# A two-layer trunk on one core: the first product of each MLP computed transposed, with the weights as stationary operand

## The chip, the core and the metric

The kernel is one launch on one core of a Trainium2 chip. It is written in Bass with the Tile framework: the program allocates tiles from pools, and a scheduler orders the instructions of each engine and places the waits between them. The engines that do the work are TensorE (PE in the profile; PEld are its weight loads), VectorE (DVE), ScalarE (ACT) and SyncE (SP), which issues the loads of the weights.

The metric is device time in microseconds (us) of the core. Before the change it is 2300.85 us, the median of three executions (2300.76 to 2300.91).

## The reference, cut to what matters

A sequence of 256 rows of 2048 numbers goes through two layers. Each layer adds the result of a mixer (attention of one kind or another) and then the result of an MLP. All is float32. The part that the change touches is the MLP with the norm ahead of it:

```python
def rms_norm(x, g):
    y = x * lax.rsqrt(jnp.mean(x * x, axis=-1, keepdims=True) + NORM_EPS)
    return y * g
...
def squared_relu_mlp(h, w1, w2):
    return jnp.square(jax.nn.relu(h @ w1)) @ w2
...
for l in range(DEPTH):
    ...
    x = x + squared_relu_mlp(rms_norm(x, mlp_norm[l]), mlp_w1[l], mlp_w2[l])
```

`DEPTH` is 2, `w1` is 2048 x 8192, `w2` is 8192 x 2048. The norm's factor, one number per row (called `rstd` below), is positive, so that it can be taken out of the relu, and its square out of the square.

## The kernel before

**Products.** All large products are made in pieces of one kind by `dense` (L189). It computes 256 rows times 512 columns of a weight matrix, over a depth given as steps `kc` of 128 (16 of them for a depth of 2048). A float32 number is split into two parts of type fp32r, a high part h and a low part l, and a product is made of three: h times h, h times l, l times h. For each step the weights arrive by DMA (`wload`, L171, two steps in one transfer), ACT casts them to `wh` (L201), and DVE subtracts to get `wl` (L202). Both come from the pool `wp` with six buffers, and are issued at high priority so that they run ahead of the matmuls.

The rows of the activation lie turned (depth on partitions), as 128x128 blocks that serve as **stationary** operand (`lhsT`); the weights, 512 columns wide, are the **moving** operand (`rhs`). For each of the two halves h of the rows there are three matmuls (L206 to L208) into one PSUM tile, so a step is six matmuls of 512 columns each, on two PSUM tiles. These come from the pool `psd`, which has four one-bank tiles; two further pools, `pst` and `psm`, have two each, for small things.

**The MLP** (`mlp`, L303) runs over four groups g. In a group four blocks b of 512 hidden columns are computed with `w1` (profile names m_0 to m_3), and then four blocks n of 512 output columns with the matching 2048 rows of `w2` (names n_0 to n_3), which are added to x (`add_to_x`, L299). Names such as `m_3h`, `n_0l` are the split weights of such a block, `m_3p` and `n_0p` their PSUM tiles. So an MLP is 32 calls of `dense`, each of 16 steps.

The result of an m block has rows on partitions, while the second product needs the hidden dimension on partitions. So ACT applies relu with the factor `rstd` (L327) and squares (L328), and the generator `spread` (L307) turns the block: 16 transposes on DVE of 32 rows each (`turn_quadrant`, L283, tile `hT`), then a cast to `hh` (L314) and a subtraction to `hl` (L315). These become the stationary operand of the n blocks, block b at steps 4b to 4b+3.

**Order.** The generators in `streams` are advanced from inside `dense`: `drip` (L182) is called once a step, and every second call takes one step of the queue "s", to which `spread` belongs. So the five pieces of `spread` are issued over about ten steps of the next block. The turned and normed input of the MLP comes from `xt_block` (L257) in two tiles, `xh` and `xl`, named xb0 to xb3 in the first layer and xd0 to xd3 in the second. `stats_end` (L252) computes `rstd`.

Of the kernel before, what the change touches and what calls it, by code (L numbers as in the profile page):

```python
# [87 lines left out]
def trunk(  # L88
# [17 lines left out]
    def tt(o, a, b, op):  # L106
        V.tensor_tensor(out=o, in0=a, in1=b, op=op)  # L107
# [4 lines left out]
    def stt(o, a, s, b, op0, op1):  # L112
        V.scalar_tensor_tensor(out=o, in0=a, scalar=s, in1=b, op0=op0, op1=op1)
# [7 lines left out]
    def act(o, a, f, scale=1.0, bias=0.0, accum=None):  # L121
        if accum is None:
            S.activation(out=o, in_=a, func=f, scale=scale, bias=bias)  # L123
        else:
            S.activation(out=o, in_=a, func=f, scale=scale, bias=bias, accum_out=accum)
# [56 lines left out]
    def drip():  # L182
# [3 lines left out]
            step("o")  # L186
        tick[0] += 1

    def dense(wsrc, stat, kcs, nm, pre=(), every=1):  # L189

        n = sum(s.shape[1] for s in wsrc)
        ps = [psd.tile([P, 512], F32, tag="d", name=f"{nm}p{h}") for h in range(NH)]
        first, last = kcs[0], kcs[-1]
        for j, kc in enumerate(kcs):
            if j % 2 == 0:
                raw = pre[j // 2] if j // 2 < len(pre) else wload(wsrc, kc, nm)
            w = raw[:, j % 2, :n]
            wh = wp.tile([P, 512], F32R, tag="wh", name=f"{nm}h{kc}")[:, :n]
            wl = wp.tile([P, 512], F32R, tag="wl", name=f"{nm}l{kc}")[:, :n]
            with tc.high_priority(offset=AHEAD):  # L200
                S.copy(wh, w)  # L201
                tt(wl, w, wh.bitcast(F32), ALU.subtract)  # L202
            for h in range(NH):
                sh, sl = stat(kc, h)
                o = ps[h][:, :n]
                E.matmul(o, lhsT=sh, rhs=wh, start=kc == first, stop=False)  # L206
                E.matmul(o, lhsT=sh, rhs=wl, start=False, stop=False)  # L207
                E.matmul(o, lhsT=sl, rhs=wh, start=False, stop=kc == last)  # L208
            if j % every == 0:
                drip()  # L210
        return ps

    def stat_of(blocks):
        def stat(kc, h):
            xh, xl = blocks[kc // 4]
            return xh[:, kc % 4, h * P:(h + 1) * P], xl[:, kc % 4, h * P:(h + 1) * P]
        return stat

    KC16 = list(range(16))
# [32 lines left out]
    def stats_end(nm):  # L252
        s = sp.tile([P, NH], F32, tag="ssq2", name=nm + "s")
        rsum(s, ssqp)
        rsqrt(rstd, s, NH, 1.0 / D, nm)

    def xt_block(xt, n, norm, nm, dst, pool=None):  # L257

        if pool is not None:
            xT = pool.tile([P, 4, T], F32, tag="hT", name=nm + "T", bufs=2)  # L260
            for i in range(4):
                turn_quadrant(xt, xT, i)
                yield
        xh = xp.tile([P, 4, T], F32R, tag="xh", name=nm + "h")
        xl = xp.tile([P, 4, T], F32R, tag="xl", name=nm + "l")
        dst.append((xh, xl))
        for c2 in range(2):
            if pool is None:
                t = quads(ps_t(f"{nm}t{c2}"), 2)
                for c in range(2):  # L270
                    for h in range(NH):
                        k = c2 * 2 + c
                        transpose(t[:, c, h * P:(h + 1) * P], xt[:, h, k * P:(k + 1) * P])
            else:
                t = xT[:, 2 * c2:2 * c2 + 2, :]
            for c in range(2):
                k = c2 * 2 + c
                g = gt[:, norm * 16 + n * 4 + k:norm * 16 + n * 4 + k + 1]
                act(xh[:, k, :], t[:, c, :], AF.Identity, scale=g)
                stt(xl[:, k, :], t[:, c, :], g, xh[:, k, :].bitcast(F32), ALU.mult, ALU.subtract)  # L280
            yield

    def turn_quadrant(src, dst, i):  # L283
# [12 lines left out]
            stats_end(nm + "e")  # L296
            yield

    def add_to_x(n, ps):  # L299
        for h in range(NH):  # L300
            tt(xs[n][:, h, :], ps[h], xs[n][:, h, :], ALU.add)

    def mlp(layer, blocks, hp, done):  # L303
        w1, w2 = mlp_w1[layer], mlp_w2[layer]
        stat = stat_of(blocks)

        def spread(r, nm, hb):  # L307
            hT = hp.tile([P, 4, T], F32, tag="hT", name=nm + "hT", bufs=2)
            for i in range(4):
                turn_quadrant(r, hT, i)  # L310
                yield
            hh = hp.tile([P, 4, T], F32R, tag="hh", name=nm + "hh")
            hl = hp.tile([P, 4, T], F32R, tag="hl", name=nm + "hl")
            S.copy(hh, hT)  # L314
            tt(hl, hT, hh.bitcast(F32), ALU.subtract)  # L315
            hb.append((hh, hl))
            yield

        for g in range(4):
            hb = []  # L320
            for b in range(4):
                nm = f"m{layer}_{g}_{b}"
                c0 = (g * 4 + b) * 512
# [12 lines left out]

# [8 lines left out]

    grow0 = sp.tile([16, P], F32, tag="junk", name="grow0")

    sp.tile([P, 96], F32, tag="fill", name="fill", bufs=1)
    warm = sp.tile([P, 512], F32, tag="junk", name="warm")
    V.memset(warm, 0.0)  # L350
    pw = ps_m("pw")
# [816 lines left out]
```

## Time and profile before

| | |
|---|---|
| median of three executions | 2300.85 us |
| the profiled execution | 2301.12 us |
| its span, first to last instruction | 2299.3 us |
| mean granted TensorE clock | 0.998 of full speed |
| matmuls recorded | 10536 |
| DMA | 426.65 MB, mean 186 GB/s |

The span has five stretches: the first mixer to 511.6 us, the first MLP to 1211.1, the second mixer to 1596.0, the second MLP to 2295.5, and the last results' way out. The two MLPs together are 1399 us of the span.

To read the profile: a row of grouped instructions gives the line, the engine, the operation, the output and the inputs by the program's names, the shape, the count, the busy time in us and the mean duration of one in ns, and then how long the engine sat idle before them and what ended that. In a row of the timeline stand the start in us, the duration in us, engine, line and operation; in brackets behind it the idle time before. The ends of matmuls are modelled and overlap, so the durations of matmuls say little: what a matmul costs is read from the distance of one start to the next.

### The profile page before, as it was taken

How to read it: one execution, taken by the hardware profiler on the slowest of the kernel's cores; microseconds unless marked ns; L12 is line 12 of the kernel's file. 1: busy time of each engine (PE TensorE's matmuls, PEld its weight loads, DVE VectorE, ACT ScalarE, POOL GpSimd, SP SyncE). 2: the span in 40 equal slices, each digit the busy share in tenths (PEclk: the TensorE clock that was granted, in tenths of full speed). 3: DMA queues.
4: the chain of work that ended last, by engine and by line, in shares of the span. 5: the costliest groups of instructions: out<-in, count | busy, mean ns of one | idle time of the engine just before them, and what ended most of it. 6: DMA issues, size and time to landing. Idle time of an engine off the chain costs nothing.

```text
span 2299.3 us, 31489 instructions
## 1 busy us (share of the span) xinstructions
PE 2280.7 (99%) x10536; PEld 1889.1 (82%) x10536; DVE 1732.9 (75%) x3539; ACT 1275.7 (55%) x2376; POOL 5.6 (0%) x15
## 2 busy tenths in 40 slices
PE   9999999999999999999999999999999999999999
PEld 8888888788888888888888888888888888888887
DVE  6768787867857857857898888987775775775774
ACT  6656756765545545545555565556554554554553
POOL 0000000000000000000000000000000000000000
PEclk9999999999999999999999999999999999999999
DMA  7655464566666666666656555555666666666665
GB/s 251 179 172 167 142 182 140 160 183 182 202 192 183 202 194 188 196 194 189 194 187 201 177 167 174 174 178 177 193 193 193 193 192 193 188 197 194 183 211 163
DMA packets 264775, 426.65 MB, mean 186 GB/s; under 512 B 22514, under 2 KB 94372, under 8 KB 264612
## 3 DMA queue, kind: packets, MB, share of 16 engines
q1 hardware_dynamic: 255812, 420.04, 59.9%
q10 hardware_dynamic: 8800, 4.60, 0.8%
q8 instruction: 82, 1.34, 0.2%
q14 instruction: 81, 0.66, 0.1%
HBM read 420.11 MB, written 4.46 MB: 185 GB/s over the span
## 4 chain that ended last, share of the span: by engine, by line
PE 84%; DVE 10%; ACT 2%; issue 2%; DMA 1%; ACTq 0%; SPq 0%; DVEq 0%
PE m_0p L208 3%; PE m_0p L206 3%; PE m_1p L208 3%; PE m_2p L208 3%; PE n_1p L208 3%; PE n_2p L208 3%; PE m_0p L207 3%; PE n_2p L207 3%; PE n_2p L206 3%; PE n_1p L207 3%; PE m_2p L207 3%; PE m_1p L206 3%; PE m_2p L206 3%; PE n_1p L206 3%; PE m_1p L207 3%; PE n_3p L208 3%
## 5 line engine op out<-in xcount | busy, mean ns | idle before, releaser
L107 DVE TENSOR_TENSOR n_3l<-n_3r,n_3h 128x512 fp32r<-128x512 f32 x128 | 88.3, 691 | 68.3 <-ACT n_3h L201 68.1
L107 DVE TENSOR_TENSOR n_2l<-n_2r,n_2h 128x512 fp32r<-128x512 f32 x128 | 88.2, 691 | 68.3 <-ACT n_2h L201 68.1
L107 DVE TENSOR_TENSOR m_0l<-m_0r,m_0h 128x512 fp32r<-128x512 f32 x128 | 88.4, 691 | 66.3 <-ACT m_0h L201 66.1
L201 ACT CAST n_3h<-n_3r 128x512 fp32r<-128x512 f32 x128 | 79.7, 623 | 89.3 <-DVE n_3l L107 73.6
L201 ACT CAST n_2h<-n_2r 128x512 fp32r<-128x512 f32 x128 | 79.7, 623 | 89.3 <-DVE n_2l L107 73.6
L107 DVE TENSOR_TENSOR n_1l<-n_1r,n_1h 128x512 fp32r<-128x512 f32 x128 | 87.0, 690 | 51.6 <-ACT n_1h L201 51.4
L201 ACT CAST m_0h<-m_0r 128x512 fp32r<-128x512 f32 x128 | 79.7, 623 | 81.8 <-DVE m_0l L107 61.8
L201 ACT CAST n_1h<-n_1r 128x512 fp32r<-128x512 f32 x128 | 78.9, 623 | 77.7 <-DVE n_1l L107 58.1
L201 ACT CAST m_1h<-m_1r 128x512 fp32r<-128x512 f32 x128 | 78.1, 622 | 64.6 <-PE m_1p L208 35.3
L107 DVE TENSOR_TENSOR m_1l<-m_1r,m_1h 128x512 fp32r<-128x512 f32 x128 | 87.1, 691 | 33.7 <-ACT m_1h L201 31.9
L201 ACT CAST m_3h<-m_3r 128x512 fp32r<-128x512 f32 x128 | 77.0, 621 | 47.0 <-PE m_3p L208 35.0
L201 ACT CAST m_2h<-m_2r 128x512 fp32r<-128x512 f32 x128 | 77.0, 621 | 46.8 <-PE m_2p L208 35.3
L201 ACT CAST n_0h<-n_0r 128x512 fp32r<-128x512 f32 x128 | 77.0, 621 | 46.5 <-PE n_0p L208 35.3
L107 DVE TENSOR_TENSOR m_3l<-m_3r,m_3h 128x512 fp32r<-128x512 f32 x128 | 84.9, 689 | 11.6 <-ACT m_3h L201 9.9
L107 DVE TENSOR_TENSOR m_2l<-m_2r,m_2h 128x512 fp32r<-128x512 f32 x128 | 84.9, 690 | 11.2 <-ACT m_2h L201 9.5
L107 DVE TENSOR_TENSOR n_0l<-n_0r,n_0h 128x512 fp32r<-128x512 f32 x128 | 84.9, 689 | 11.0 <-ACT n_0h L201 9.2
L289 DVE STREAM_TRANSPOSE m_0hT<-m_0r 32x256 f32<-32x256 f32 x128 | 55.8, 436 | 10.5 <-ACT m_0r L123 8.0
L289 DVE STREAM_TRANSPOSE m_1hT<-m_1r 32x256 f32<-32x256 f32 x128 | 55.8, 436 | 10.4 <-ACT m_1r L123 7.9
L289 DVE STREAM_TRANSPOSE m_3hT<-m_3r 32x256 f32<-32x256 f32 x128 | 55.8, 436 | 10.4 <-ACT m_3r L123 7.9
L289 DVE STREAM_TRANSPOSE m_2hT<-m_2r 32x256 f32<-32x256 f32 x128 | 55.8, 436 | 10.4 <-ACT m_2r L123 7.9
L208 PE MATMUL n_0p<-n_0h,m_3hl 128*128 128x512 f32 x64 | 25.8, 404 | 1.9 <-DVE m_3hl L107 1.9
L206 PE MATMUL n_0p<-n_0h,m_3hh 128*128 128x512 f32 x64 | 25.0, 390 | 0.0
(2552 smaller groups left out, 7389.0 us busy)
## 6 DMA issues: line engine op xcount, KB each, us to landing
m_0r<-in_mlp_w_dram SPq DMA_DIRECT2D x64, 512.0 KB
m_1r<-in_mlp_w_dram SPq DMA_DIRECT2D x64, 512.0 KB
m_2r<-in_mlp_w_dram SPq DMA_DIRECT2D x64, 512.0 KB
m_3r<-in_mlp_w_dram SPq DMA_DIRECT2D x64, 512.0 KB
n_0r<-in_mlp_w_dram SPq DMA_DIRECT2D x64, 512.0 KB
n_1r<-in_mlp_w_dram SPq DMA_DIRECT2D x64, 512.0 KB
n_2r<-in_mlp_w_dram SPq DMA_DIRECT2D x64, 512.0 KB
n_3r<-in_mlp_w_dram SPq DMA_DIRECT2D x64, 512.0 KB
```

The lines of the kernel that those rows point to most:

```text
L107: V.tensor_tensor(out=o, in0=a, in1=b, op=op)
L201: S.copy(wh, w)
L206: E.matmul(o, lhsT=sh, rhs=wh, start=kc == first, stop=False)
L207: E.matmul(o, lhsT=sh, rhs=wl, start=False, stop=False)
L208: E.matmul(o, lhsT=sl, rhs=wh, start=False, stop=kc == last)
L289: V.transpose(out=dv[:, :, :, q], in_=sv[:, :, :, j, :])
```

## The change

The first product of each MLP no longer goes through `dense` but through a new function, `hidden`. In it the weights are the stationary operand: a step's 512 columns of `w1` are four blocks of 128, and the activation is the moving operand. Its high and low parts lie side by side in one tile now (`xhl`, high and low 256 columns each), so that one matmul of 512 columns gives a weight block's high part times both, into the two halves of a PSUM tile, and a second one of 256 columns adds the low part of the weights times the high part of the activation. A step is therefore four matmuls of 512 columns and four of 256, on four PSUM tiles, one for each 128 hidden columns. The result has the hidden dimension on partitions, so `spread` and its transposes are gone. The two halves of each PSUM tile are added (a copy on ACT and an addition on DVE for each), then relu, square, cast and subtraction follow.

The factor of the norm now belongs to columns of that result and cannot be applied there by a per-partition scale. It is left out there; its square, `rstd2`, is applied where the second product is added to x, as a scalar of the same DVE instruction. Blocks with even b take all four tiles of `psd`, those with odd b the two of `pst` and the two of `psm`. The split of the weights is moved into a function of its own, `split`, with the same instructions.

```diff
+    def split(raw, j, n, nm):
+        w = raw[:, j % 2, :n]
+        wh = wp.tile([P, 512], F32R, tag="wh", name=nm + "h")[:, :n]
+        wl = wp.tile([P, 512], F32R, tag="wl", name=nm + "l")[:, :n]
+        with tc.high_priority(offset=AHEAD):
+            S.copy(wh, w)
+            tt(wl, w, wh.bitcast(F32), ALU.subtract)
+        return wh, wl
...
+    rstd2 = cp.tile([P, NH], F32, name="rstd2")
...
         rsqrt(rstd, s, NH, 1.0 / D, nm)
+        if nm.startswith(("xb", "xd")):
+            tt(rstd2, rstd, rstd, ALU.mult)
...
-        xh = xp.tile([P, 4, T], F32R, tag="xh", name=nm + "h")
-        xl = xp.tile([P, 4, T], F32R, tag="xl", name=nm + "l")
-        dst.append((xh, xl))
+        xhl = xp.tile([P, 4, 2, T], F32R, tag="x", name=nm + "x")
+        dst.append(xhl)
...
+    def add_to_x(n, ps, scale=None):
         for h in range(NH):
-            tt(xs[n][:, h, :], ps[h], xs[n][:, h, :], ALU.add)
+            x = xs[n][:, h, :]
+            if scale is None:
+                tt(x, ps[h], x, ALU.add)
+            else:
+                stt(x, ps[h], scale[:, h:h + 1], x, ALU.mult, ALU.add)
+
+    def hidden(w1, blocks, b, hp, nm):
+        if b % 2 == 0:
+            ps = [psd.tile([P, 512], F32, tag="d", name=f"{nm}p{i}") for i in range(4)]
+        else:
+            ps = [f(f"{nm}p{i}") for i, f in enumerate((ps_t, ps_t, ps_m, ps_m))]
+        ps = [quads(p, 2) for p in ps]
+        for j, kc in enumerate(KC16):
+            if j % 2 == 0:
+                raw = wload([w1[:, b * 512:(b + 1) * 512]], kc, nm)
+            wh, wl = split(raw, j, 512, f"{nm}_{kc}")
+            xk = blocks[kc // 4][:, kc % 4]
+            for fb in range(4):
+                E.matmul(ps[fb], lhsT=wh[:, fb * P:(fb + 1) * P], rhs=xk, start=kc == 0, stop=False)
+            for fb in range(4):
+                E.matmul(ps[fb][:, 0, :], lhsT=wl[:, fb * P:(fb + 1) * P], rhs=xk[:, 0, :], start=False, stop=kc == 15)
+            drip()
+        r = hp.tile([P, 4, T], F32, tag="hr", name=nm + "r", bufs=2)
+        for fb in range(4):
+            S.copy(r[:, fb, :], ps[fb][:, 1, :])
+            tt(r[:, fb, :], ps[fb][:, 0, :], r[:, fb, :], ALU.add)
+        act(r, r, AF.Relu)
+        act(r, r, AF.Square)
+        hb = hp.tile([P, 4, 2, T], F32R, tag="hb", name=nm + "hb")
+        S.copy(hb[:, :, 0, :], r)
+        tt(hb[:, :, 1, :], r, hb[:, :, 0, :].bitcast(F32), ALU.subtract)
+        return hb
...
-                ps = dense([w1[:, c0:c0 + 512]], stat, KC16, nm)
-                r = hp.tile([P, NH, 512], F32, tag="hr", name=nm + "r", bufs=2)
-                for h in range(NH):
-                    act(r[:, h, :], ps[h], AF.Relu, scale=rstd[:, h:h + 1])
-                act(r, r, AF.Square)
-                streams["s"].append(spread(r, nm, hb))
-            hstat = stat_of(hb)
+            hstat = stat_of([hidden(w1, blocks, g * 4 + b, hp, f"m{layer}_{g}_{b}") for b in range(4)])
...
-                add_to_x(n, ps)
+                add_to_x(n, ps, rstd2)
```

Three places show what stands on the engines now. The first is PE in the first layer's block m0_0_1, step 4. Before, `m0_0_1p0` and `p1` are the PSUM tiles of the two halves of the rows, `m0_0_1h4` and `l4` the split weights (moving), `xb1h` and `xb1l` the activation (stationary):

```order
L206 MATMUL m0_0_1p0_6072<-m0_0_1h4_6129,xb1h_5641 128x512
L207 MATMUL m0_0_1p0_6072<-m0_0_1l4_6130,xb1h_5641 128x512
L208 MATMUL m0_0_1p0_6072<-m0_0_1h4_6129,xb1l_5642 128x512
L206 MATMUL m0_0_1p1_6073<-m0_0_1h4_6129,xb1h_5641 128x512
L207 MATMUL m0_0_1p1_6073<-m0_0_1l4_6130,xb1h_5641 128x512
L208 MATMUL m0_0_1p1_6073<-m0_0_1h4_6129,xb1l_5642 128x512
```

Of the change, the same step on PE (`xb1x` is the activation, both parts; `m0_0_1_4h` and `_4l` are the split weights):

```order
L329 MATMUL m0_0_1p0_6110<-xb1x_5637,m0_0_1_4h_6168 128x512
L329 MATMUL m0_0_1p1_6111<-xb1x_5637,m0_0_1_4h_6168 128x512
L329 MATMUL m0_0_1p2_6112<-xb1x_5637,m0_0_1_4h_6168 128x512
L329 MATMUL m0_0_1p3_6113<-xb1x_5637,m0_0_1_4h_6168 128x512
L331 MATMUL m0_0_1p0_6110<-xb1x_5637,m0_0_1_4l_6169 128x256
L331 MATMUL m0_0_1p1_6111<-xb1x_5637,m0_0_1_4l_6169 128x256
L331 MATMUL m0_0_1p2_6112<-xb1x_5637,m0_0_1_4l_6169 128x256
L331 MATMUL m0_0_1p3_6113<-xb1x_5637,m0_0_1_4l_6169 128x256
```

Six matmuls of 512 columns, 3072 in all, have become four of 512 and four of 256, again 3072, and every one has a weight load of its own. This is so in all 512 steps of the m blocks (two layers, 16 blocks, 16 steps); the steps of the n blocks keep the first form.

The second place is PE at the change from a group to the next, in the first layer. Of the change, from the last matmul of `n0_0_3` on (`xb0x` is the activation's first block, `m0_1_0p0` to `p3` are the four tiles of `psd`):

```order
L212 MATMUL n0_0_3p1_7329<-n0_0_3_15h_7496,m0_0_3hb_6785 128x512
L329 MATMUL m0_1_0p0_7508<-xb0x_5522,m0_1_0_0h_7514 128x512
L329 MATMUL m0_1_0p1_7509<-xb0x_5522,m0_1_0_0h_7514 128x512
L331 MATMUL m0_1_0p0_7508<-xb0x_5522,m0_1_0_0l_7515 128x256
L331 MATMUL m0_1_0p1_7509<-xb0x_5522,m0_1_0_0l_7515 128x256
L329 MATMUL m0_1_0p0_7508<-xb0x_5522,m0_1_0_1h_7526 128x512
L329 MATMUL m0_1_0p2_7510<-xb0x_5522,m0_1_0_0h_7514 128x512
L331 MATMUL m0_1_0p2_7510<-xb0x_5522,m0_1_0_0l_7515 128x256
L329 MATMUL m0_1_0p1_7509<-xb0x_5522,m0_1_0_1h_7526 128x512
L329 MATMUL m0_1_0p2_7510<-xb0x_5522,m0_1_0_1h_7526 128x512
L329 MATMUL m0_1_0p3_7511<-xb0x_5522,m0_1_0_0h_7514 128x512
```

`p2` and `p3` take the two banks that `n0_0_3` has just filled, and the scheduler has put five and nine other matmuls ahead of their first ones. Before, a block needed two banks, and those were the two that `n0_0_2` had left.

The third place is DVE at the end of the last m block of a group, while the first n block runs. Before, up to the low part of that block (`m0_0_3hT` is the block being turned, `m0_0_3hl` its low part, `n0_0_0l11` to `l13` the low parts of the n block's weights; the first transposes stand behind `n0_0_0l5`):

```order
L289 STREAM_TRANSPOSE m0_0_3hT_6705<-m0_0_3r_6677 32x2x4x32 x2
L107 TENSOR_TENSOR n0_0_0l11_6827<-n0_0_0r10_6814,n0_0_0h11_6826 128x512
L289 STREAM_TRANSPOSE m0_0_3hT_6705<-m0_0_3r_6677 32x2x4x32 x3
L107 TENSOR_TENSOR n0_0_0l12_6839<-n0_0_0r12_6836,n0_0_0h12_6838 128x512
L289 STREAM_TRANSPOSE m0_0_3hT_6705<-m0_0_3r_6677 32x2x4x32 x2
L107 TENSOR_TENSOR n0_0_0l13_6849<-n0_0_0r12_6836,n0_0_0h13_6848 128x512
L107 TENSOR_TENSOR m0_0_3hl_6811<-m0_0_3hT_6705,m0_0_3hh_6810 128x1024
```

Of the change, from the n block's split of step 5 on, on DVE (`m0_0_3p0` to `p3` are the block's PSUM tiles, `m0_0_3r` the sum, `m0_0_3hb` its split):

```order
L107 TENSOR_TENSOR n0_0_0_5l_6847<-n0_0_0r4_6834,n0_0_0_5h_6846 128x512
L107 TENSOR_TENSOR m0_0_3r_6774<-m0_0_3p0_6562,m0_0_3r_6774 128x256
L107 TENSOR_TENSOR m0_0_3r_6774<-m0_0_3p1_6563,m0_0_3r_6774 128x256
L107 TENSOR_TENSOR m0_0_3r_6774<-m0_0_3p2_6564,m0_0_3r_6774 128x256
L107 TENSOR_TENSOR m0_0_3r_6774<-m0_0_3p3_6565,m0_0_3r_6774 128x256
L107 TENSOR_TENSOR n0_0_0_6l_6859<-n0_0_0r6_6856,n0_0_0_6h_6858 128x512
L107 TENSOR_TENSOR n0_0_0_7l_6869<-n0_0_0r6_6856,n0_0_0_7h_6868 128x512
L107 TENSOR_TENSOR n0_0_0_8l_6881<-n0_0_0r8_6878,n0_0_0_8h_6880 128x512
L107 TENSOR_TENSOR m0_0_3hb_6785<-m0_0_3r_6774,m0_0_3hb_6785 128x4x256
```

The low part of the last block, which the n block's steps 12 to 15 need, stood behind the split of step 13 and now stands behind that of step 8. Outside the MLPs the order on PE and SP is the one of before.

More of the change, by code (lines that the diff above doesn't have):

```diff
@@ L196, in dense @@
                 raw = pre[j // 2] if j // 2 < len(pre) else wload(wsrc, kc, nm)
[L197 to L202, printed above, removed]
+            wh, wl = split(raw, j, n, f"{nm}_{kc}")
             for h in range(NH):
@@ L214, in stat @@
         def stat(kc, h):
-            xh, xl = blocks[kc // 4]
-            return xh[:, kc % 4, h * P:(h + 1) * P], xl[:, kc % 4, h * P:(h + 1) * P]
+            return tuple(blocks[kc // 4][:, kc % 4, s, h * P:(h + 1) * P] for s in range(2))
         return stat
@@ L278, in xt_block @@
                 g = gt[:, norm * 16 + n * 4 + k:norm * 16 + n * 4 + k + 1]
-                act(xh[:, k, :], t[:, c, :], AF.Identity, scale=g)
-                stt(xl[:, k, :], t[:, c, :], g, xh[:, k, :].bitcast(F32), ALU.mult, ALU.subtract)
+                act(xhl[:, k, 0, :], t[:, c, :], AF.Identity, scale=g)
+                stt(xhl[:, k, 1, :], t[:, c, :], g, xhl[:, k, 0, :].bitcast(F32), ALU.mult, ALU.subtract)
             yield
@@ L303, in mlp @@
     def mlp(layer, blocks, hp, done):
         w1, w2 = mlp_w1[layer], mlp_w2[layer]
[L305 to L317, printed above, removed]
@@ L319, in mlp @@
-        for g in range(4):
[L320 to L323, printed above, removed]
-                ps = dense([w1[:, c0:c0 + 512]], stat, KC16, nm)
-                r = hp.tile([P, NH, 512], F32, tag="hr", name=nm + "r", bufs=2)
-                for h in range(NH):
-                    act(r[:, h, :], ps[h], AF.Relu, scale=rstd[:, h:h + 1])
-                act(r, r, AF.Square)
-                streams["s"].append(spread(r, nm, hb))
-            hstat = stat_of(hb)
+        for g in range(4):
+            hstat = stat_of([hidden(w1, blocks, g * 4 + b, hp, f"m{layer}_{g}_{b}") for b in range(4)])
@@ L346, in trunk @@
     grow0 = sp.tile([16, P], F32, tag="junk", name="grow0")
-    sp.tile([P, 96], F32, tag="fill", name="fill", bufs=1)
+    sp.tile([P, 88], F32, tag="fill", name="fill", bufs=1)
     warm = sp.tile([P, 512], F32, tag="junk", name="warm")
```

1 line of the change is left out of this document (removed).

## The prediction

> **What bounds the kernel now.** I read the page first: the busy line and the chain, then a table by stage for the two MLPs, then the timeline of PE inside them.
>
> ```profile
> PE 2280.7 (99%) x10536; PEld 1889.1 (82%) x10536; DVE 1732.9 (75%) x3539; ACT 1275.7 (55%) x2376; POOL 5.6 (0%) x15
> ...
> PE 84%; DVE 10%; ACT 2%; issue 2%; DMA 1%; ACTq 0%; SPq 0%; DVEq 0%
> ```
>
> PE is busy 99% of the span and carries 84% of the chain that ended last. The stages:
>
> ```profile
> 511.60:1211.10 699.50, 698.55 (x3081) 577.16 (x3081) 520.83 (x893) 373.46 (x608) 0.00 (x0) 1.00 0.63 192
> ...
> 1596.00:2295.50 699.50, 698.53 (x3081) 576.96 (x3079) 494.33 (x829) 362.76 (x579) 0.00 (x0) 1.00 0.63 191
> ```
>
> These are the two MLPs: length in us, then PE, PEld, DVE, ACT and POOL busy, the granted clock (1.00) and the DMA share. PE fills all but 1 us of 699.5, while DVE is busy 74% or 71% and ACT 53%. Since a busy PE need not be PE at its pace, I look at the starts of successive matmuls.
>
> ```profile
> 999.76 0.39 PE L206 MATMUL n_2p<-n_2h,m_1hh 128*128 128x512 f32 x1
> ...
> 1005.88 0.39 PE L206 MATMUL n_2p<-n_2h,m_2hh 128*128 128x512 f32 x1
> ```
>
> There are 27 starts from the first row to the second (not counting the first), so 6.12 / 27 = **226.7 ns** for a matmul of 512 columns with its weight load. An MLP has 32 blocks of 96 such matmuls: 3072 x 226.7 ns = 696.4 us. It takes 699.5, so 3.1 us are anything else. The MLP is a stream of matmuls at its pace. What the change takes from DVE and ACT shows in the time only where it ends a wait of PE; what it does to the count and width of the matmuls shows in full.
>
> **The change, part by part.** The sum is made against the profiled execution, 2301.12 us (1.8 us outside its span of 2299.3), which lies 0.3 us above the median of 2300.85.
>
> *1. The matmuls of the m blocks.* There are 2 x 16 x 16 = 512 steps. Each had 6 x 226.7 = 1360 ns. Now it has four matmuls of 512 columns and four of 256. No fp32r matmul of 256 columns is in the trace. The nearest are those of 264 columns in the first mixer:
>
> ```profile
> 42.22 0.28 PE L207 MATMUL z2p<-z2l,xa1h 128*128 128x264 f32 x1
> ...
> 44.86 0.28 PE L208 MATMUL z2p<-z2h,xa2l 128*128 128x264 f32 x1
> ```
>
> 22 starts in 2.64 us: **120.0 ns** each, again with a weight load for every matmul. Half of 226.7 would be 113.3, so a narrow matmul costs more per column. What 256 columns cost is bounded so: 113.3 ns if the cost is in proportion to the columns; 116.6 on the line through the two rows (106.7 ns for 248 columns, 0.430 ns a column); 120.0 if a short matmul has a floor of which 8 columns more or less are no part. I take the nearest row, 120.0. A step then takes 4 x 226.7 + 4 x 120.0 = 1386.7 ns, 26.7 more than now, and 512 of them **+13.7 us**. By the other two values it is 0 and +6.6 us.
>
> The upper end comes from what happens where the width changes:
>
> ```profile
> 49.46 0.39 PE L206 MATMUL bv0p<-bv0h,xa0h 128*128 128x512 f32 x1
> 49.68 0.40 PE L207 MATMUL bv0p<-bv0l,xa0h 128*128 128x512 f32 x1
> 49.92 0.40 PE L208 MATMUL bv0p<-bv0h,xa0l 128*128 128x512 f32 x1
> 50.15 0.40 PE L206 MATMUL bv0p<-bv0h,xa0h 128*128 128x512 f32 x1
> 50.39 0.39 PE L207 MATMUL bv0p<-bv0l,xa0h 128*128 128x512 f32 x1
> ```
>
> These are the first wide matmuls behind the 264-column ones: four starts in 0.93 us, 233 ns each, where the settled pace is 226.7. In the changed step the width alternates every four matmuls, so the wide ones may never settle. Then a step takes 4 x 233 + 4 x 120 = 1412 ns, 52 more than now, and the term is +26.6 us.
>
> A rule speaks on this. The Trainium skill, page "TensorE: Matmul & The Clock Gate", section "Back-to-back issue gap", gives a warm matmul N/2.4 + 2.5 ns: a fixed part for each matmul beside its columns, so that more matmuls for the same columns cost more. That is the direction of this change, and the two rows show it too. The size that the Trainium skill gives is another: by it 512 columns take 215.8 ns and 264 take 112.5, where the trace has 226.7 and 120.0; its step would grow by 5 ns, the term by an estimated 2.6 us.
>
> *2. The wait of the first n block for the last m block.* Once in each group PE waits:
>
> ```profile
> 616.22 0.39 PE L207 MATMUL n_0p<-n_0l,m_3hh 128*128 128x512 f32 x1
> 616.84 0.50 PE L208 MATMUL n_0p<-n_0h,m_3hl 128*128 128x512 f32 x1 [0.24 <-DVE m_3hl L107]
> 617.18 0.39 PE L206 MATMUL n_0p<-n_0h,m_3hh 128*128 128x512 f32 x1
> 617.41 0.39 PE L207 MATMUL n_0p<-n_0l,m_3hh 128*128 128x512 f32 x1
> 617.64 0.40 PE L208 MATMUL n_0p<-n_0h,m_3hl 128*128 128x512 f32 x1
> 617.88 0.39 PE L206 MATMUL n_0p<-n_0h,m_3hh 128*128 128x512 f32 x1
> ```
>
> From 616.22 to 617.88 are five matmuls, 5 x 226.7 = 1.13 us; it took 1.66. So 0.53 us are lost, in eight groups 4.2 us. The low part of the turned block comes late, since `spread` is handed out a piece every second step. What follows the last matmul of the block now: four copies and four additions out of PSUM, relu, square, a cast, a subtraction. The nearest rows:
>
> ```profile
> L123 ACT ACTIVATE xb2h<-xb2t,gt 128x256 fp32r<-128x256 f32 x4 | 1.9, 473 | 1.6 <-DVE xb2l L113 1.6
> L123 ACT ACTIVATE m_3r<-m_3r 128x1024 f32<-128x1024 f32 x8 | 8.5, 1061 | 0.3
> L314 ACT CAST m_3hh<-m_3hT 128x1024 fp32r<-128x1024 f32 x8 | 8.4, 1053 | 24.8 <-DVE m_3hT L289 24.8
> ...
> L201 ACT CAST m_3h<-m_3r 128x512 fp32r<-128x512 f32 x128 | 77.0, 621 | 47.0 <-PE m_3p L208 35.0 <-PE m_2p L208 10.7 <-DMA m_3r<-in_mlp_w_dram 1.3
> ...
> L107 DVE TENSOR_TENSOR m_3hl<-m_3hT,m_3hh 128x1024 fp32r<-128x1024 f32 x8 | 9.8, 1225 | 3.2 <-ACT m_3hh L314 3.2
> ```
>
> ACT: 4 x 0.47 for the copies, 2 x 1.06 for relu and square, 1.05 for the cast, and three casts of weights that stand between them, 3 x 0.62: 6.9 us. With one addition on DVE (about 0.48, as the copy) and the subtraction of 1.23 it is 8.6 us. The n block reaches step 12 after 12 x 1.36 = 16.3 us. So the wait goes, **-4.2 us**, and nothing of this chain is next to be late: PE's own matmuls are. If the chain were about twice as long, the wait would come back, +4.2.
>
> *3. The PSUM banks.* A block with even b needs all four tiles of `psd`. At the start of a group two of them are those that the last n block filled. Before, DVE empties them so:
>
> ```profile
> 687.36 1.28 DVE L107 TENSOR_TENSOR xs<-n_3p,xs 128x512 f32<-128x512 f32 x2
> ```
>
> while on PE the last n matmul and the first m matmul start at
>
> ```profile
> 687.02 0.39 PE L208 MATMUL n_3p<-n_3h,m_3hl 128*128 128x512 f32 x1
> 687.25 0.39 PE L206 MATMUL m_0p<-m_0h,xb0h 128*128 128x512 f32 x1
> ```
>
> The additions end at about 688.0 and 688.6. In the new order three wide and two narrow matmuls stand ahead of the first use of the third bank: 687.25 + 0.92 = 688.17; the fourth is used four matmuls later, at 688.97. Both are free by then: 0. If another subtraction of 0.69 us slips ahead on DVE, the third bank comes about 0.5 us late, in eight groups up to 4 us. Blocks with odd b use `pst` and `psm`, whose other users are done by then, and every later pair of blocks has a whole block (21.8 us) for emptying.
>
> *4. What else goes and comes.* Of DVE's work the 16 transposes of a block go:
>
> ```profile
> L289 DVE STREAM_TRANSPOSE m_0hT<-m_0r 32x256 f32<-32x256 f32 x128 | 55.8, 436 | 10.5 <-ACT m_0r L123 8.0
> ```
>
> That is 7.0 us a block, 223 us in 32 blocks, and none of it is time: PE's 21.8 us a block cover it. The four additions (about 1.9 us) and ACT's four copies in place of two relus out of PSUM lie under the same cover. The factor at `add_to_x` rides in an instruction that is there; `rstd2` is one short instruction in each layer. At the very end the last two additions get a scalar, at most some 0.1 us. The split weights now feed PE's weight loads, which therefore wait for them; the row of the casts `m_3h` above shows ACT idle most often because PE has not yet freed a buffer, so the splits are ahead of PE, and the wait is 0. Transfers and their order stay.
>
> Sum: 2301.1 + 13.7 - 4.2 + 0 = **2310.6 us**, +0.42% on the median.
>
> **Rivals.**
>
> *A. The narrow matmuls cost little or nothing extra* (the other side). At 113.3 ns the step stays 1360 and the wait's end is all that is left: 2301.1 - 4.2 = 2296.9. On the line, at 116.6, it is 2303.5. For it: 256 is half of 512, and 264 is not a round width. It decides at (1360 + 16.9 - 906.8) / 4 = 117.5 ns a narrow matmul; below this the time is no longer slower by over 0.2%. Against it: no row shows a short fp32r matmul below 120 on average. The Trainium skill's small fixed part would give an estimated 2299.5, in this case's range.
>
> *B. The wide matmuls never settle.* Then 2301.1 + 26.6 - 4.2 = 2323.5. For it: the 233 ns above. Against it: alternating at a regular beat may settle in a pattern of its own.
>
> *C. The narrow ones run at the rate of plain f32.* Of 256 columns the trace has only such:
>
> ```profile
> 1278.05 0.59 PE L1078 MATMUL e0po<-e0pT,vc 128*128 128x256 f32 x2
> 1278.48 0.38 PE L1079 MATMUL e0po<-e0pT,vc 128*128 128x128 f32 x2
> ```
>
> Two in 0.43 us, 215 ns each. That would be a step of 1767 ns and 2505 us. The 264-column rows, of the same type as the new ones, speak against it.
>
> *D. The change doesn't free the first n block*: the wait stays, 2314.8. It lies in the forecast's own range.
>
> **How the numbers follow.** The forecast with D and late banks (2307 to 2316) has 0.43; A 0.30, of which 0.05 for a narrow matmul cheaper still than 113.3 or some gain not seen; B 0.24; C and the rest 0.03. About 0.2%, 4.6 us, is what a measurement of this kernel can tell from no change. Faster by more (below 2296.2): 0.05. Within (2296.2 to 2305.5): 0.26. Slower by more: 0.69. The range goes from A's lower end, 2297, to B's 2324; it leaves out C, what lies beyond B, and gains beyond A.
>
> **What would show it.** In the changed profile: starts of four wide and four narrow matmuls in an m block, 1387 ns for a step (1360 to 1373 for A, about 1412 for B); no idle time ahead of the n_0 matmuls that read the last block; no wait of PE at a group's first block; PE still above 98% and DVE's busy time some 160 us lower. A step below 1376 ns, or waits of PE for wh or wl, which now feed its weight loads, would make the prediction wrong.

## The result, and the profile after

The changed kernel takes **2318.23 us** (median of four executions, 2317.46 to 2318.91), beside 2300.88 us for the kernel before on the same chip (2300.76 to 2301.88). The ratio is 1.0076, 95% interval 1.0064 to 1.0088: slower by 17.3 us. The forecast was 2310.6 in a range of 2297 to 2324, so the sign and the range held, and 7.6 us are missing from the sum. The time lies above the band that the prediction gave its own forecast (2307 to 2316) and nearer to rival B's 2323.5: the range held because it reached up to B. The profiled execution of the changed kernel took 2318.91 us with a span of 2317.1, which is 17.8 us longer than before.

The page of after, the busy line and the chain that ended last:

```profile
PE 2299.6 (99%) x11560; PEld 1939.9 (84%) x11560; DVE 1566.1 (68%) x3157; ACT 1300.9 (56%) x2472; POOL 5.6 (0%) x15
...
PE 88%; DVE 7%; DMA 2%; ACT 1%; issue 1%; ACTq 0%; SPq 0%; DVEq 0%
```

The binding engine is the same, and its share of the chain has grown from 84 to 88%. 1024 matmuls are more (two in each of 512 steps), as the order said. DVE lost 166.8 us of work and ACT gained 25; neither shows in the time. The two MLPs by stage, after (length, then PE, PEld, DVE, ACT and POOL busy):

```profile
511.51:1220.18 708.67, 708.67 (x3594) 603.10 (x3593) 437.40 (x702) 386.13 (x657) 0.00 (x0) 1.00 0.61 190
1604.89:2313.60 708.71, 708.42 (x3591) 602.68 (x3590) 410.91 (x638) 375.13 (x627) 0.00 (x0) 1.00 0.60 189
```

Together they are 1417.4 us where they were 1399.0: all of the 17.8 us, and 0.6 more that the rest gives back. The granted clock is 1.00, as before, so nothing of it is throttling. What the time went into is seen in a steady m block. The timeline of PE there has one row for four matmuls in sequence (start, duration of the four with their modelled ends):

```profile
558.27 1.09 PE L329 MATMUL m_2p<-xb0x,m_1h 128*128 128x512 f32 x4
559.20 0.64 PE L331 MATMUL m_2p<-xb0x,m_1l 128*128 128x256 f32 x4
559.67 1.09 PE L329 MATMUL m_2p<-xb0x,m_2h 128*128 128x512 f32 x4
560.60 0.63 PE L331 MATMUL m_2p<-xb0x,m_2l 128*128 128x256 f32 x4
561.08 1.09 PE L329 MATMUL m_2p<-xb0x,m_3h 128*128 128x512 f32 x4
562.00 0.64 PE L331 MATMUL m_2p<-xb0x,m_3l 128*128 128x256 f32 x4
562.48 1.09 PE L329 MATMUL m_2p<-xb1x,m_4h 128*128 128x512 f32 x4
```

From 558.27 to 562.48 are three steps: 1403 ns each, where the forecast had 1387. From each wide row to the narrow one behind it are 0.93, 0.93 and 0.92 us, 232 ns a matmul; from each narrow row to the next wide one 0.47, 0.48 and 0.48, 119 ns. PE has no idle time in any of these rows. The starts of single matmuls repeat over two steps: 235, 233, 236, 224 ns for wide ones, 118, 120, 120, 120 for narrow ones, then 233, 236, 228, 233 and 117, 119, 118, 117; that is 1403.3 ns a step on average, and 512 steps are 22.2 us longer than at 1360.

The wait of the first n block has gone. The same place in after, with the low part of the last block on DVE and step 12 on PE, from two timelines:

```profile
608.22 1.23 DVE L107 TENSOR_TENSOR m_3hb<-m_3r,m_3hb 128x1024 fp32r<-128x1024 f32 x1 [0.26 <-ACT m_3hb L340]
```

```profile
618.12 0.39 PE L210 MATMUL n_0p<-n_12h,m_3hb 128*128 128x512 f32 x1
618.35 0.39 PE L211 MATMUL n_0p<-n_12l,m_3hb 128*128 128x512 f32 x1
618.58 0.39 PE L212 MATMUL n_0p<-n_12h,m_3hb 128*128 128x512 f32 x1
```

The block is ready at 609.45, its first reader starts at 618.12, and the matmuls go by at 227 ns.

### The profile page after: what moved, and what is told of

Same layout as the page of the kernel before. It is cut to its first block, busy times and chain, and to the rows that moved or that the text cites. A ratio compares the mean times of both kernels' runs of the same rounds, so it can differ in the third digit from the quotient of the medians.

```text
span 2317.1 us, 33506 instructions
## 1 busy us (share of the span) xinstructions
PE 2299.6 (99%) x11560; PEld 1939.9 (84%) x11560; DVE 1566.1 (68%) x3157; ACT 1300.9 (56%) x2472; POOL 5.6 (0%) x15
## 4 chain that ended last, share of the span: by engine, by line
PE 88%; DVE 7%; DMA 2%; ACT 1%; issue 1%; ACTq 0%; SPq 0%; DVEq 0%
PE m_0p L329 5%; PE m_3p L329 5%; PE m_2p L329 5%; PE m_1p L329 5%; PE m_1p L331 3%; PE m_2p L331 3%; PE m_3p L331 3%; PE m_0p L331 3%; PE n_0p L212 3%; PE n_0p L211 3%; PE n_2p L212 3%; PE n_1p L212 3%; PE n_0p L210 3%; PE n_2p L210 3%; PE n_1p L210 3%; PE n_1p L211 3%
## 5 line engine op out<-in xcount | busy, mean ns | idle before, releaser
L123 ACT ACTIVATE m_3r<-m_3r 128x1024 f32<-128x1024 f32 x16 | 16.9, 1059 | 1.8 <-DVE m_3r L107 1.8
L123 ACT ACTIVATE m_0r<-m_0r 128x1024 f32<-128x1024 f32 x16 | 16.9, 1056 | 0.0
L123 ACT ACTIVATE m_1r<-m_1r 128x1024 f32<-128x1024 f32 x16 | 16.9, 1055 | 0.0
L123 ACT ACTIVATE m_2r<-m_2r 128x1024 f32<-128x1024 f32 x16 | 16.9, 1055 | 0.0
L113 DVE SCALAR_TENSOR_TENSOR xs<-n_3p,rstd,xs 128x512 f32<-128x512 f32 x16 | 11.3, 744 | 6.1 <-PE n_3p L212 6.1
L107 DVE TENSOR_TENSOR m_0r<-m_0p,m_0r 128x256 f32<-128x256 f32 x32 | 12.0, 418 | 0.0
L107 DVE TENSOR_TENSOR m_2r<-m_2p,m_2r 128x256 f32<-128x256 f32 x32 | 12.0, 418 | 0.0
L107 DVE TENSOR_TENSOR m_1r<-m_1p,m_1r 128x256 f32<-128x256 f32 x32 | 12.0, 417 | 0.0
L107 DVE TENSOR_TENSOR m_3r<-m_3p,m_3r 128x256 f32<-128x256 f32 x32 | 11.3, 417 | 0.0
L113 DVE SCALAR_TENSOR_TENSOR xs<-n_2p,rstd,xs 128x512 f32<-128x512 f32 x16 | 11.2, 744 | 0.0
```

## The experiments

Three theories of the missing 7.6 us stood against each other. W: narrow matmuls cost 120.0 ns and wide ones 226.7 when they are among their like, and it is the change of width that makes the wide ones behind it slower. M: the narrow matmul is simply dearer, (1403.3 - 906.8) / 4 = 124.1 ns. S: weights as stationary operand make matmuls dearer, whatever their width. Changes are against the changed kernel unless said otherwise.

### All matmuls of the m blocks 256 wide

```diff
-                E.matmul(ps[fb], lhsT=wh[:, fb * P:(fb + 1) * P], rhs=xk, start=kc == 0, stop=False)
+                for s in range(2):
+                    E.matmul(ps[fb][:, s, :], lhsT=wh[:, fb * P:(fb + 1) * P], rhs=xk[:, s, :], start=kc == 0 and s == 0,
+                             stop=False)
```

> The changed kernel, its m blocks made of 256-column matmuls alone: 12 in a step, the same 3072 columns, the same result. Theory W (the price is in the change of width; among themselves narrow matmuls settle): if they settle at 113.3 ns, half of a wide one, a step takes 1360 ns and the kernel about 2296 us; if they settle at 120 ns, as the 264-column ones did, 1440 ns and 2337 us. Theory M (every matmul more costs a fixed 43.3 / 2 = 21.7 ns, whatever stands beside it): six more than before, 1490 ns and 2363 us.

2338.26 us (2337.11 to 2339.43), ratio to before 1.0166 (1.0151 to 1.0181); the kernel before took 2299.40 us beside this run and the next three. The timeline of PE in this run:

```profile
558.98 1.12 PE L330 MATMUL m_2p<-xb0x,m_0h 128*128 128x256 f32 x8
559.94 0.64 PE L333 MATMUL m_2p<-xb0x,m_0l 128*128 128x256 f32 x4
560.42 1.12 PE L330 MATMUL m_2p<-xb0x,m_1h 128*128 128x256 f32 x8
```

Twelve matmuls in 1.44 us: 120.0 ns, and every single one of a block has it. The price that the prediction took from 264-column rows is that of 256 columns, with the weights stationary. M fell.

### The old orientation, with the low part's products cut in two

This is the kernel before with four wide and four narrow matmuls in an m step, and the weights still moving:

```diff
...
+            if nm.startswith("m"):
+                for h in range(NH):
+                    sh, sl = stat(kc, h)
+                    E.matmul(ps[h], lhsT=sh, rhs=wh, start=kc == first, stop=False)
+                    E.matmul(ps[h], lhsT=sl, rhs=wh, start=False, stop=False)
+                for h in range(NH):
+                    sh, sl = stat(kc, h)
+                    for c in range(2):
+                        cs = slice(c * 256, c * 256 + 256)
+                        E.matmul(ps[h][:, cs], lhsT=sh, rhs=wl[:, cs], start=False, stop=kc == last and c == 1)
...
```

> The kernel before, orientation unchanged; in the m blocks only the products with the weights' low part are cut into two matmuls of 256 columns each, and a step is ordered as four wide and four narrow, as in the changed kernel. Same result. Theories W and M, both: the same 1403 ns a step, 512 x 43 ns = +22 us on 2300.9, so about 2323 us. Theory S (the price comes from the weights as stationary operand, whose loads now read freshly written tiles): the cut alone costs little, 1360 to 1373 ns a step, 2301 to 2308 us.

2321.96 us (2320.67 to 2322.63), ratio 1.0095 (1.0080 to 1.0110). The timeline of PE:

```profile
558.04 0.40 PE L206 MATMUL m_2p<-m_2h,xb0h 128*128 128x512 f32 x1
...
558.97 0.64 PE L212 MATMUL m_2p<-m_2l,xb0h 128*128 128x256 f32 x4
559.45 0.40 PE L206 MATMUL m_2p<-m_2h,xb0h 128*128 128x512 f32 x1
```

Four wide ones (the first of them and three left out) take 0.93 us, four narrow ones 0.48: the changed kernel's step, without its orientation. S fell. What this run keeps is the wait, by the list of PE's waits:

```profile
PE n_0p L219 <- DVE m_3hl L107: 2.4, 8, 0.3
```

So its eight first n blocks are 4.8 us longer than those of the changed kernel, and its m blocks 1.0 us shorter: the time is the changed kernel's with that wait on top.

### Wide and narrow in turn

```diff
                 E.matmul(ps[fb], lhsT=wh[:, fb * P:(fb + 1) * P], rhs=xk, start=kc == 0, stop=False)
-            for fb in range(4):
                 E.matmul(ps[fb][:, 0, :], lhsT=wl[:, fb * P:(fb + 1) * P], rhs=xk[:, 0, :], start=False, stop=kc == 15)
```

> The changed kernel with the order inside a step alone changed: wide and narrow in turn (512, 256, 512, 256, ...). Theory W: every wide matmul follows a narrow one; either none settles, 4 x 235 + 4 x 118 = 1412 ns a step and 2323 us, or the regular pair settles at 226.7 + 120, 1387 ns and 2310 us. In any case the time is another than 2318. Theory M: same matmuls, same 1403 ns, 2318 us.

2316.72 us (2315.05 to 2319.15), ratio 1.0070 (1.0053 to 1.0087). The time can't be told from the changed kernel's, though W expected another, but the trace can. The first wide matmul of steps 0 and 4 of block m_2, in the first group and in the second:

```profile
558.25 0.39 PE L329 MATMUL m_2p<-xb0x,m_0h 128*128 128x512 f32 x1
...
563.80 0.39 PE L329 MATMUL m_2p<-xb1x,m_4h 128*128 128x512 f32 x1
...
734.99 0.40 PE L329 MATMUL m_2p<-xb0x,m_0h 128*128 128x512 f32 x1
...
740.64 0.40 PE L329 MATMUL m_2p<-xb1x,m_4h 128*128 128x512 f32 x1
```

Four steps take 5.55 us in the one, 1387 ns each, and 5.65 in the other, 1413 each. The same instructions run in two rhythms: four groups keep the first through their blocks m_1 to m_3, the other four the second. Their mean, 1400 ns, is next to the changed kernel's 1403, so the time hides them. The first has the length of the sum of settled prices, though its wide ones stand 230 ns and its narrow ones 117 ns ahead of the next; the second is what the prediction's rival B gave. No fixed price of an instruction can do that; M has none to offer.

### Sixteen wide, then sixteen narrow

```diff
+        held = []
...
-            for fb in range(4):
-                E.matmul(ps[fb][:, 0, :], lhsT=wl[:, fb * P:(fb + 1) * P], rhs=xk[:, 0, :], start=False, stop=kc == 15)
+            held.append((wl, xk, kc))
+            if j % 4 == 3:
+                for l, y, k in held:
+                    for fb in range(4):
+                        E.matmul(ps[fb][:, 0, :], lhsT=l[:, fb * P:(fb + 1) * P], rhs=y[:, 0, :], start=False, stop=k == 15)
+                held = []
```

> The changed kernel with the narrow matmuls of four steps put together: 16 wide, then 16 narrow. Theory W: the wide ones lose about 48 ns once in 16 (as behind the 264-column ones in the first mixer) and then run at 226.7, the narrow ones run at 120: 906.7 + 12 + 480 = 1399 ns a step, 2316 us; if the narrow ones settle at 113.3, 1372 ns and 2302 us. Theory M: 1403 ns, 2318 us. The traces' starts tell more than the time here: under W the last six of 16 wide ones are 226.7 ns apart, under M all are about 232.

2311.88 us (2310.97 to 2312.92), ratio 1.0052 (1.0037 to 1.0067). The timeline of PE:

```profile
561.48 1.09 PE L330 MATMUL m_2p<-xb1x,m_4h 128*128 128x512 f32 x4
562.41 1.07 PE L330 MATMUL m_2p<-xb1x,m_5h 128*128 128x512 f32 x4
563.32 1.07 PE L330 MATMUL m_2p<-xb1x,m_6h 128*128 128x512 f32 x4
564.23 1.07 PE L330 MATMUL m_2p<-xb1x,m_7h 128*128 128x512 f32 x4
565.13 0.64 PE L335 MATMUL m_2p<-xb1x,m_4l 128*128 128x256 f32 x4
```

The four behind the change take 0.93 us, the next twelve 0.91, 0.91 and 0.90: they settle. The same matmuls in another order take 1391.7 ns a step in place of 1403.3, and the kernel is 12.5 us above the one before in place of 17.3. So the excess hangs on how often the width changes, and W holds. The size was missed: 1399 ns a step were expected. Against settled prices a group of four steps loses 4 x (1391.7 - 1386.7) = 20 ns here for one pair of changes, where the changed kernel loses 16.6 ns for one.

### All matmuls of the m blocks 512 wide

```diff
-                E.matmul(ps[fb][:, 0, :], lhsT=wl[:, fb * P:(fb + 1) * P], rhs=xk[:, 0, :], start=False, stop=kc == 15)
+                E.matmul(ps[fb], lhsT=wl[:, fb * P:(fb + 1) * P], rhs=xk, start=False, stop=kc == 15)
```

> The changed kernel with the second matmuls of a step 512 columns wide too (the low part of the weights times both parts of the activation, so that the product of the two low parts is added, which the reference has too): eight wide matmuls a step, weights still stationary. Theory W (price in the change of width): all settle at 226.7, 8 x 226.7 = 1813 ns a step, 453 more than 1360, so 2301 - 4.2 + 232 = 2529 us. Theory S' (weights as stationary operand cost something of their own, hidden in the mix): more than 1813, 8 x 232 = 1856 ns and 2551 us.

2526.72 us in one execution (before 2299.94). The timeline of PE:

```profile
558.38 1.07 PE L329 MATMUL m_1p<-xb2x,m_11h 128*128 128x512 f32 x4
559.28 1.07 PE L331 MATMUL m_1p<-xb2x,m_11l 128*128 128x512 f32 x4
560.19 1.07 PE L329 MATMUL m_1p<-xb3x,m_12h 128*128 128x512 f32 x4
561.10 1.07 PE L331 MATMUL m_1p<-xb3x,m_12l 128*128 128x512 f32 x4
```

Twelve in 2.72 us: 226.7 ns, as in the kernel before. A dearer wide matmul in the new orientation is ruled out. Each width has its settled price there, and a step of the mixture costs 16.6 ns more than the sum of both.

### The old kernel, the last block turned sooner

The kernel before, with one more piece of `spread` handed out in each step of the first n block:

```diff
+            if fast:
+                step("s")
...
+                           fast=n == 0)
```

> The kernel before, all matmuls as they were; in the first n block of each group the queue of the turning pieces gets one more piece a step, so that the last m block is turned earlier. It does alone what the change did to the wait. Theory: the 0.53 us lost at n_0's step 12 in each of eight groups go, nothing else changes: 2300.9 - 4.2 = 2296.7 us, ratio 0.998, and in the trace n_0 blocks of 21.76 to 21.8 us in place of 22.3. Rival: another wait of the same size takes its place, 2300.9.

2295.80 us (2293.00 to 2297.47, 11 executions) beside 2299.94 (2297.53 to 2301.50, 15), ratio **0.9981** (0.9972 to 0.9990). PE at the place of the wait:

```profile
616.51 0.39 PE L207 MATMUL n_0p<-n_0l,m_3hh 128*128 128x512 f32 x1
616.74 0.39 PE L208 MATMUL n_0p<-n_0h,m_3hl 128*128 128x512 f32 x1
616.97 0.39 PE L206 MATMUL n_0p<-n_0h,m_3hh 128*128 128x512 f32 x1
```

The matmul that waited 0.24 us starts 0.23 behind the one ahead of it, and every block but the first of each MLP now takes 21.76 us. The wait's worth is 4.1 us by the medians, 4.3 by the lengths of the eight blocks. This version beats both kernels: the one gain of the change can be had without its orientation.

### All matmuls of the m blocks 128 wide

```diff
-                E.matmul(ps[fb], lhsT=wh[:, fb * P:(fb + 1) * P], rhs=xk, start=kc == 0, stop=False)
+                for s in range(2):
+                    for c in (slice(0, P), slice(P, T)):
+                        E.matmul(ps[fb][:, s, c], lhsT=wh[:, fb * P:(fb + 1) * P], rhs=xk[:, s, c],
+                                 start=kc == 0 and s == 0 and c.start == 0, stop=False)
```

> The changed kernel, its m blocks made of 128-column matmuls alone, 24 in a step, same columns and result. If a matmul among equals costs 13.3 ns beside its columns (line through 226.7 at 512 and 120.0 at 256: 0.4167 ns a column), 128 columns cost 66.7 ns: 1600 ns a step, 240 more, 2301 - 4.2 + 123 = 2420 us. If 120 ns is a floor for any short matmul (set by its weight load), 24 x 120 = 2880 ns a step and 3075 us.

The low part's products are cut in the same way. 2970.77 us in one execution (before 2299.94), and both expected numbers were wrong. In a window of 80 us PE issues 719 matmuls, some 111 ns each (111.7 by the starts in the m blocks):

```profile
560.00:640.00 80.00, 80.00 (x719) 80.00 (x718) 24.20 (x39) 23.65 (x41) 0.00 (x0) 1.00 0.35 100
```

Half the columns save 8 ns of 120, so something other than the columns sets most of the pace of short matmuls. The next four runs ask whether it is the load of the weights; they cut it in half, three of them by columns and one by rows.

### Half a weight load, mixed widths and 256 alone

```diff
+            m = P if kc in (0, 15) else 64
...
-                E.matmul(ps[fb], lhsT=wh[:, fb * P:(fb + 1) * P], rhs=xk, start=kc == 0, stop=False)
+                E.matmul(ps[fb][:m], lhsT=wh[:, fb * P:fb * P + m], rhs=xk, start=kc == 0, stop=False)
```

The low part's products are cut in the same way, and the second run has this on top of the 256-wide kernel.

> The changed kernel, but in steps 1 to 14 of an m block each matmul loads only 64 of its 128 columns of weights and writes 64 rows; the moving operands stay 512 and 256 wide, in the same order. This leaves out half of the hidden columns in these steps. Theory C (the pace of a matmul, and its slowness behind a change of width, come from the columns that stream): the step stays at 1403 ns with the same two series of starts (about 235, 233, 236, 224 and 118, 120, 120, 120), 2318 us. Theory L (the weight load sets the 120 ns of a narrow matmul and disturbs the next wide one): with loads of half the size the narrow ones fall to 113 ns or less and the wide ones to 227 or less, the step to 1360 or less; 448 of the 512 steps are changed, so the time falls by 448 x 0.043 = 19 us or more, to 2299 or less.

> The run with all matmuls of the m blocks 256 wide (12 in a step, 120.0 ns each, 2338 us), but with half-size weight loads in steps 1 to 14, which leaves out half of the hidden columns there. Theory C (the 120 ns belong to 256 columns): 120.0 ns again, step 1440, 2338 us. Theory L (they belong to the weight load): the pace falls, to 113 ns if the columns' own share in proportion is next (step 1360, 2338 - 448 x 0.08 = 2302 us), lower if it is less than that.

The mixed one took 2306.11 us and the 256-wide one 2305.89 (one execution each, before 2300.68). The timeline of PE in the 256-wide one, and two rows of its weight loads by shape (count, busy us, mean ns of one):

```profile
564.14 1.07 PE L331 MATMUL m_2p<-xb1x,m_4h 128*64 128x256 f32 x8
565.04 0.62 PE L334 MATMUL m_2p<-xb1x,m_4l 128*64 128x256 f32 x4
565.50 1.07 PE L331 MATMUL m_2p<-xb1x,m_5h 128*64 128x256 f32 x8
```

```profile
L331 PEld LDWEIGHTS m_0p<-xb0x,m_1h 128*64 128x64 f32 x32 | 3.9, 135 | 0.0
...
L331 PEld LDWEIGHTS m_2p<-xb0x,m_0h 128*128 128x128 f32 x32 | 4.1, 192 | 0.0
```

The load is 57 ns shorter, and twelve matmuls take 1.36 us: **113.3 ns** instead of 120.0, L's number. The total is 4 us above L's 2302, in a single execution; 0.5 us of that are in the MLPs. So the last 6.7 ns of a narrow matmul hang on the columns of weights that are loaded, or on the rows that are written to PSUM, which the same edit halves; no run here separates these two. The mixed one's timeline:

```profile
559.37 1.08 PE L330 MATMUL m_2p<-xb0x,m_2h 128*64 128x512 f32 x4
560.29 0.62 PE L332 MATMUL m_2p<-xb0x,m_2l 128*64 128x256 f32 x4
560.75 1.08 PE L330 MATMUL m_2p<-xb0x,m_3h 128*64 128x512 f32 x4
```

A step is 1.38 us here (1373.3 over the block), neither C's 1403 nor L's 1360. Narrow ones take 0.46 us for four, but the wide ones still 0.91 to 0.92, 229 each on average: the same cut makes the wide ones cheaper behind the change, but doesn't settle them.

### Half a load, 512 alone; half the depth, 256 alone

The first is the 512-wide run with the same cut. The second is the 256-wide run with all columns and half of the rows:

```diff
+                    E.matmul(ps[fb][:, s, :], lhsT=wh[:m, fb * P:(fb + 1) * P], rhs=xk[:m, s, :],
+                             start=kc == 0 and s == 0, stop=False)
```

> The run with all matmuls of the m blocks 512 wide (8 in a step, 226.7 ns each, 2526.7 us), but with 64 columns of weights loaded in place of 128 in steps 1 to 14, which leaves out half of the hidden columns there. In the 256-wide run the same cut took the pace from 120.0 to 113.3 ns. If the 13 ns that a matmul costs beyond its columns belong to the weight load whatever the width, the wide ones fall by the same 6.7 ns to 220.0: 448 x 8 x 0.0067 = 24 us, 2503 us. If a wide matmul hides its load altogether, they stay at 226.7, 2527 us.

> The 256-wide run again, with the other half left out: in steps 1 to 14 the weights are loaded for all 128 columns but only 64 of the 128 rows of the depth (half of the sum is left out there). If what counts is the size of the load, 113.3 ns as with 64 columns, and 2306 us. If it is the number of columns loaded (or of rows written to PSUM), 120.0 ns and 2338 us.

The 512-wide one took 2540.48 us (before 2302.17, one execution each): dearer than with full loads, which neither number allowed. PE there:

```profile
561.38 1.08 PE L332 MATMUL m_1p<-xb2x,m_11l 128*64 128x512 f32 x4
562.30 1.09 PE L330 MATMUL m_1p<-xb3x,m_12h 128*64 128x512 f32 x4
563.23 1.08 PE L332 MATMUL m_1p<-xb3x,m_12l 128*64 128x512 f32 x4
564.14 1.08 PE L330 MATMUL m_1p<-xb3x,m_13h 128*64 128x512 f32 x4
```

Twelve in 2.76 us, 230 each, with starts between 224 and 236 that repeat and never settle. There is no change of width in this run. So the unsettled rhythm of wide matmuls is not bound to a change of width alone; 226.7 is a rhythm that equal matmuls with full loads fall into. Here too half of the rows written go with half of the load.

The half-depth one took 2353.32 us. Its timeline and its loads:

```profile
561.01 1.12 PE L331 MATMUL m_2p<-xb0x,m_2h 64*128 64x256 f32 x8
561.97 0.40 PE L334 MATMUL m_2p<-xb0x,m_2l 64*128 64x256 f32 x2
```

```profile
L331 PEld LDWEIGHTS m_0p<-xb0x,m_3h 64*128 64x128 f32 x32 | 4.1, 188 | 0.0
```

Eight in 0.96 us, 120.0 ns, and loads of 188 ns: of the two answers on record it is the columns loaded (or the rows written), not the size of the load. The 15 us above the expected 2338 come with the changes between full and half depth: four steps of a block beside them, the first two and the last two, take 1526 to 1531 ns instead of 1440, and the blocks m_0, in which steps overlap, lose more. The Trainium skill, page "TensorE: Matmul & The Clock Gate", section "LDWEIGHTS (loading the stationary operand)", says of the time of a load that "it's the 128 columns that matter", not the depth, and gives 1/1.2 ns a column. Both runs agree: half the columns shorten the recorded load by 57 ns (its figure makes 53, an estimate), half the depth hardly at all. The recorded loads as such are longer than its figure, 192 ns where it makes an estimated 107.

## Why the prediction came out so

Between the two profiled executions:

| step | forecast, us | measured, us |
|---|---|---|
| 1 and 3, the m blocks | +13.7 + 0 | +22.4 |
| 2, the first n block of each group | -4.2 | -4.0 |
| 4, and what lies outside the MLPs | 0 | -0.6 |
| span | +9.5 | +17.8 |

**Step 1** had the sign and one of two costs: 13.7 us forecast, 22.2 measured in the steps. What it had right is that a narrow matmul costs more than half of a wide one; what it left out of the sum is the change of width. "A step then takes 4 x 226.7 + 4 x 120.0 = 1386.7 ns" added prices that each hold among their like. The narrow one was right: 120.0 in the 256-wide run, and the 512-wide run has 226.7 in the new orientation. In the mixture the wide ones cost 232 and the narrow ones 119 (232.3 and 118.55 on average): 4 x 5.6 - 4 x 1.45 = +16.6 ns a step, 8.5 us. The prediction had this as rival B, at 233 ns from rows behind a change of width, and gave it 0.24; the wide half of B came true, while the narrow ones gave 1.45 ns each back, which B did not have. B's time is 5.3 us off and the forecast's 7.6, so the rival with the smaller chance came nearer. The old-orientation run shows that nothing else of the change is needed for it. The argument against B, that a regular beat may settle in a pattern of its own, was true and proved nothing: the pattern is regular, and it is a dear one. In the alternating run either outcome occurred. The formula of the Trainium skill that the prediction set beside its sum (page "TensorE: Matmul & The Clock Gate", section "Back-to-back issue gap") is given there as the "isolated single-MM gap", not for a stream of matmuls with their loads; the 2299.5 us estimated from it are 18.7 too low.

**Rival A** decided at 117.5 ns for a narrow matmul; with 120.0 it fell. Of the streams of 256 columns alone only the one with 64-column loads came under that point. In the alternating run the narrow ones stand at 116.4 ns on average, but the wide ones beside them at 233.6, so that no step there is below 1386 ns; A needed one below 1376. **Rival C** (215 ns) and **D** (the wait stays) fell.

**Step 2** was right: the wait of 0.53 us in eight groups was put at 4.2 us; the blocks that had it take 21.79 to 21.81 us instead of 22.3, and the last block is ready 7.7 us after its m block ends, where the forecast had 8.6. The run on the old kernel confirms the price on its own.

**Step 3** was put at 0, with up to 4 us if another subtraction slipped ahead of the additions on DVE. One stands just ahead of them, but it didn't hold them up. DVE and PE of after at the start of the second group:

```profile
688.34 0.69 DVE L107 TENSOR_TENSOR m_4l<-m_0r,m_4h 128x512 fp32r<-128x512 f32 x1 [0.67 <-ACT m_4h L194]
688.95 1.40 DVE L113 SCALAR_TENSOR_TENSOR xs<-n_3p,rstd,xs 128x512 f32<-128x512 f32 x2
```

```profile
688.61 0.39 PE L212 MATMUL n_3p<-n_15h,m_3hb 128*128 128x512 f32 x1
...
689.76 0.48 PE L329 MATMUL m_0p<-xb0x,m_0h 128*128 128x512 f32 x1
690.08 0.28 PE L331 MATMUL m_0p<-xb0x,m_0l 128*128 128x256 f32 x1
```

The additions start 0.34 us behind the last matmul of n_3, at 688.95 behind 688.61, and so they did before, at 687.36 behind 687.02. Of their 1.40 us about half goes by until the third bank is free, at some 689.65, and its first use is at 689.76. The wide matmul there is followed after 0.32 us in place of 0.23, so at most 0.09 us was lost; the first blocks of the later groups are 0.05 us longer than the other m blocks, 0.3 us in six. The five matmuls put ahead were cover enough.

**Step 4** was right: DVE lost 167 us (forecast 160) and the time gained nothing, since PE had covered it; the list of PE's waits names no m or n block and no split weights.

## What to carry to other kernels

A matmul's price read from a run of equal matmuls holds only there: when an edit mixes widths on an engine that is busy throughout, look for rows just behind a change of width and price the mixture by them, and keep equal widths together (sixteen and sixteen lost 5 ns a step where four and four lost 16.6). Work taken off an engine that waits, 167 us of it here, is worth only the wait that ends with it; find that wait first, as it may go by an edit of a few lines.

## What the runs showed that was not expected

- The pace of a stream of equal matmuls does not follow the columns: 226.7 ns for 512, 120.0 for 256, 111.7 for 128, with full weight loads.
- Loading 64 columns in place of 128, and so writing 64 rows, takes the 256-wide ones to 113.3 ns, and spoils the 512-wide ones, 226.7 to 230. Why the wide ones do not settle there stays open.
- Behind a change of width the wide ones need five matmuls to settle in the sixteen-and-sixteen run, and ten in the kernel before behind the 264-column ones: 2.31 us for the ten from 49.46 us on, then 226.7 ns each. What in PE keeps them unsettled so long stays open.
- The same alternating instructions ran at 1387 ns a step in four groups and at 1413 in four others of one execution.
